# Seven block products for eight in the down product's middle twelve K tiles

## The chip, the cores and the metric

The kernel runs on one core of one Trainium2 chip. The metric is the device time of one execution in microseconds, given as the median of several runs. The profile is one execution taken by the hardware profiler. PE is the matrix engine (TensorE), DVE the vector engine, ACT the scalar engine, POOL the GpSimd engine, and SP the engine that issues all transfers here, in one queue.

## The reference

One layer of an encoder over 1088 tokens (64 sample tokens and 1024 of a prompt): a combined projection, windowed attention beside a state-space mixer, an output projection and LN1, and then a gated feed-forward part and LN2. The change lies in the feed-forward part:

```
h = layer_norm(DN_ALPHA * x + mix, ln1_g, ln1_b)
g, up = jnp.split(h @ w_gate_up, 2, axis=-1)
f = (jax.nn.silu(g) * up) @ w_down
y = layer_norm(DN_ALPHA * h + f, ln2_g, ln2_b)
```

The model width is 1024 (8 tiles of 128 features), the hidden width 2816 (22 tiles of 128). Everything is fp32.

## The kernel before, in words

Features lie on the 128 partitions and tokens on the free axis; the 1088 tokens are four chunks of 272 (`QN`). To keep fp32 accuracy every operand is split into h, its rounding to the matrix engine's fp32r format (a copy on ACT), and l, the rest (a subtraction on DVE, both in `split`, line 1307). A product is then three matmuls, h x h, h x l and l x h (`mm3`, line 758, and `acc3`).

Nothing is issued as the program text has it. All instructions are recorded by `Plan` (from line 90), with the row buffers and banks that they use. `order` (line 285) then writes each engine's queue: of the instructions that are ready by its cost table it takes the earliest, and among those the one of the lowest priority number, which grows with the place in the text (times `step`) and falls with the cost of all that hangs on it. `plan.base` shifts that number. The queues are fixed after that, and an instruction waits in its queue for what it needs.

Buffers: `R` hands out 21 row buffers of 1088 words, `W` ten weight buffers of 1024 words, `R4` four big buffers of four rows each, and `PM` the eight PSUM banks.

The gate/up stage (`gu_load`, line 1372, and `gu_mm`, line 1405) already uses seven products for eight: a hidden tile's gate and up weights, each cut into two halves of four K tiles, are the 2x2 blocks of the left side, and h, cut by the same halves and by pairs of token chunks, those of the right. h is mixed once (`h_mix`, line 1330); its products 7, 6 and 4 keep twelve row buffers to the end of the stage. The weights are mixed per tile: `ws` and `wt` hold the sums s1 to s4, and of u's second half `wd` is made. The product order is 1, 5, 2, 7, 3, 6, 4 (`ORDER`), each for the chunk pairs s = 0 and 1. Products 1 and 2 share bank A, 5 and 3 bank D, 7 and 4 bank C. The tile's activation `act` is stored to DRAM (`ascr`), 22 in all.

The down stage runs over K in four blocks of 5, 5, 4 and 8 hidden tiles (`DN_BLOCKS`, line 39). `act_load` (line 1449) reads the activations back and splits them. For each of eight output tiles `mo` and four chunks `c`, `down` (line 1463) sums its K tiles in one bank, and one DVE instruction adds the bank to the result f (in the queues: `g0_0` and so on, chunk and feature half), which begins as ALPHA times h.

The last block runs chunk by chunk, so that LN2 of a chunk (`fm_norm`, line 1197) goes beside the matmuls of the next. For chunk c it sums over features with `mu` and `va` on PE, and spreads the scale over the partitions with three matmuls `rp` (`spread`, line 1190). Chunk 3 has its own end (`fm_tail`, line 1227): it subtracts a mean of the first five feature tiles (`shl`), adds the other three tiles' products to that, and forms the statistics `dcl` (mean by token), `del` (the same, spread) and `val` (squares) in pieces:

```
        plan.base = TAILB
        token_rows(dc, ds, True, False)
        PE.matmul(de[:, 0:n], omean, ds, start=True, stop=False)
        token_rows(va, B, True, False)
        token_rows(dc, d[7], False, True)
        token_rows(va, q[7], False, True)
        PE.matmul(de[:, 0:n], omean, d[7], start=False, stop=True)
```

Here ds is the sum of d[5] and d[6], made by DVE, and B the sum of the squares q[0] to q[6], made by POOL; both lie in the buffer `ntl`.

Of the kernel before, what the change touches and what calls it, by code (L numbers as in the profile page):

```python
# [10 lines left out]
F32 = mybir.dt.float32  # L11
# [27 lines left out]
DN_BLOCKS = [5, 5, 4, 8]  # L39
# [50 lines left out]
class Plan:  # L90
# [194 lines left out]
    def order(self):  # L285
# [13 lines left out]
        step = 1.1 * sum(o.cost for o in ops if o.eng == "PE") / n  # L299
# [121 lines left out]
def layer(ctx: ExitStack, tc: tile.TileContext, I, O):  # L421
# [13 lines left out]
    def R(dt, name, words=1088):  # L435
        return own(row.tile([128, words], dt, tag="R", name=name), "R", NR)
# [68 lines left out]
    ascr = [DT([128, T], f"ascr{m}") for m in range(DFF_T)]  # L505
    kscr = DT([16, 32, 128], "kscr")
# [720 lines left out]
    def fm_tail(c, gg, bbias, step):  # L1227
# [41 lines left out]
        token_rows(va, q[7], False, True)  # L1269
        PE.matmul(de[:, 0:n], omean, d[7], start=False, stop=True)  # L1270
# [100 lines left out]
    @plan.part  # L1371
    def gu_load(m):
        g, u = R(F32, f"wg{m}"), R(F32, f"wu{m}")
        for i, t in enumerate((g, u)):
            SP.dma_start(t[:, 0:1024], I["w_gu"][2 * m + i].rearrange("p a b -> p (a b)"))
        a11, a12, a21, a22 = g[:, 0:512], g[:, 512:1024], u[:, 0:512], u[:, 512:1024]
        sa, sb = R(F32, f"ws{m}"), R(F32, f"wt{m}")
        s1, s2, s3, s4 = sa[:, 0:512], sa[:, 512:1024], sb[:, 0:512], sb[:, 512:1024]
        V.tensor_tensor(s1, a21, a22, op=ALU.add)
        V.tensor_tensor(s2, s1, a11, op=ALU.subtract)  # L1380
        V.tensor_tensor(s3, a11, a21, op=ALU.subtract)
        V.tensor_tensor(s4, a12, s2, op=ALU.subtract)
# [22 lines left out]
    def gu_mm(m, subs):  # L1405
# [36 lines left out]
        if 1 in subs:  # L1442
            SP.dma_start(ascr[m], act)
# [4 lines left out]
    @plan.part  # L1448
    def act_load(m0, nb, big):
        for i in range(nb):  # L1450
            a = R(F32, f"ar{m0 + i}")
            SP.dma_start(a, ascr[m0 + i])
            if big:
                if i % 2 == 0:
                    t_ = R4(F32R, f"ah{m0 + i}")
                h, l = t_[:, 2 * (i % 2)], t_[:, 2 * (i % 2) + 1]
            else:
                h, l = R(F32R, f"ah{m0 + i}"), R(F32R, f"al{m0 + i}")
            split(a, h, l)
            ACT_[m0 + i] = (h, l)  # L1460

# [109 lines left out]
    m0 = 0  # L1571
    for bi, nb in enumerate(DN_BLOCKS):
        act_load(m0, nb, bi % 2 == 1)
        if bi + 1 < len(DN_BLOCKS):
            for mo in range(8):
                down(m0, nb, bi == 0, mo, dn_load(m0, nb, mo))
        else:
            wd = [dn_load(m0, nb, mo, W if mo < 4 else RW) for mo in range(8)]
            for c in range(4):
                if c == 3:  # L1580
                    fm_tail(c, g2, b2, lambda k, f: down(m0, nb, False, k, wd[k], (c,), f))
                    break
                for mo in range(8):
                    down(m0, nb, False, mo, wd[mo], (c,))
                fm_norm(1, c, g2, b2, ln2_out)
        m0 += nb
# [94 lines left out]
```

## Time and profile before

| what | us |
|---|---|
| runs (three) | 1162.64 to 1166.91, median 1166.75 |
| the profiled execution's own time | 1167.67 |
| its span on the core | 1165.9 |
| PE busy | 1121.4 |
| DVE busy | 758.0 |
| ACT busy | 488.2 |

The span is the time from the first to the last instruction of the core; some 1.8 us of the execution lie around it. The mean granted clock of PE is 0.986 of full speed. A matmul's record lasts longer than the distance to the next one, since matmuls are pipelined, so durations of PE are read as distances between starts.

### The profile page before, as it was taken

How to read it: one execution, taken by the hardware profiler on the slowest of the kernel's cores; microseconds unless marked ns; L12 is line 12 of the kernel's file. 1: busy time of each engine (PE TensorE's matmuls, PEld its weight loads, DVE VectorE, ACT ScalarE, POOL GpSimd, SP SyncE). 2: the span in 40 equal slices, each digit the busy share in tenths (PEclk: the TensorE clock that was granted, in tenths of full speed). 3: DMA queues.
4: the chain of work that ended last, by engine and by line, in shares of the span. 5: the costliest groups of instructions: out<-in, count | busy, mean ns of one | idle time of the engine just before them, and what ended most of it. 6: DMA issues, size and time to landing. Idle time of an engine off the chain costs nothing.

```text
span 1165.9 us, 21135 instructions
## 1 busy us (share of the span) xinstructions
PE 1121.4 (96%) x8595; PEld 1093.7 (94%) x8595; DVE 758.0 (65%) x1550; ACT 488.2 (42%) x989; POOL 78.6 (7%) x123
## 2 busy tenths in 40 slices
PE   5998898999999999999999999999999999999996
PEld 5998788798799999999999999999999999999995
DVE  7999995677866998564645646556447353743554
ACT  5557345785832565243333333333334121410334
POOL 1101012123310010000000000000000000000012
PEclk8999999999999999999999999999999999999997
DMA  9455578420120322141131221311367161410112
GB/s 298 112 151 159 165 224 243 124 86 10 39 76 14 112 95 94 56 167 56 56 112 56 87 80 56 111 56 69 120 211 244 35 230 46 154 38 1 40 39 77
DMA packets 73721, 122.50 MB, mean 105 GB/s; under 512 B 11974, under 2 KB 49416, under 8 KB 73608
## 3 DMA queue, kind: packets, MB, share of 16 engines
q1 hardware_dynamic: 73624, 121.16, 32.1%
q8 instruction: 67, 1.10, 0.4%
q14 instruction: 30, 0.25, 0.1%
HBM read 84.08 MB, written 38.24 MB: 105 GB/s over the span
## 4 chain that ended last, share of the span: by engine, by line
PE 62%; DVE 2%; POOL 1%; DMA 0%; issue 0%; ACT 0%; POOLq 0%; DVEq 0%; ACTq 0%
PE dn L417 22%; PE guA L417 10%; PE guD L417 10%; PE guC L417 10%; PE guB L417 5%; PE gp L417 3%; DVE dl L417 1%; DVE f L417 1%; DMA ar<-ascr 0%; POOL rs L417 0%; PE rp L417 0%; DVE nt L417 0%; POOL ntl L417 0%; PE val L417 0%; PE mu L417 0%
## 5 line engine op out<-in xcount | busy, mean ns | idle before, releaser
L417 PE MATMUL guA<-hc,wah 128*128 128x272 f32 x640 | 127.1, 288 | 0.0
L417 DVE TENSOR_TENSOR tm<-tm 128x272 f32<-128x272 f32 x80 | 35.0, 438 | 122.5 <-ACT tm L417 122.5
L417 PEld LDWEIGHTS guA<-hc,wah 128*128 128x128 f32 x640 | 100.5, 188 | 0.0
L417 PE MATMUL guA<-hc,wal 128*128 128x272 f32 x320 | 92.4, 289 | 0.0
L417 DVE TENSOR_TENSOR g<-g,dn 128x272 f32<-128x272 f32 x93 | 40.1, 435 | 78.4 <-PE dn L417 78.0
L417 PE MATMUL guC<-hh,wd 128*128 128x272 f32 x320 | 64.0, 289 | 0.0
L417 PE MATMUL guD<-hc,wch 128*128 128x272 f32 x320 | 63.1, 287 | 0.0
L417 PE MATMUL guD<-hc,wbh 128*128 128x272 f32 x320 | 62.8, 289 | 0.0
L417 PEld LDWEIGHTS guA<-hc,wal 128*128 128x128 f32 x320 | 60.2, 188 | 0.0
L417 POOL TENSOR_TENSOR rs<-rs,nhalf 128x3 f32<-128x3 f32 x7 | 7.8, 1113 | 772.2 <-DVE rs L417 772.2
L417 PEld LDWEIGHTS guC<-hh,wd 128*128 128x128 f32 x320 | 51.6, 188 | 0.0
L417 DVE TENSOR_TENSOR wcl<-wt,wch 128x1024 fp32r<-128x1024 f32 x20 | 24.5, 1225 | 39.9 <-PE guD L417 38.2
L417 PEld LDWEIGHTS guD<-hc,wbh 128*128 128x128 f32 x320 | 50.4, 188 | 0.0
L417 PEld LDWEIGHTS guD<-hc,wch 128*128 128x128 f32 x320 | 50.2, 188 | 0.0
L417 ACT ACTIVATE act<-guA 128x272 f32<-128x272 f32 x40 | 15.9, 397 | 79.5 <-PE guA L417 79.5
L417 PE MATMUL guD<-hc,wbl 128*128 128x272 f32 x160 | 46.4, 290 | 0.0
L417 PE MATMUL guB<-hl,wbh 128*128 128x272 f32 x160 | 46.3, 289 | 0.0
L417 PE MATMUL guC<-hl,wd 128*128 128x272 f32 x160 | 46.2, 289 | 0.0
L417 PE MATMUL guC<-hl,wch 128*128 128x272 f32 x160 | 46.2, 289 | 0.0
L417 PE MATMUL guB<-hh,wbl 128*128 128x272 f32 x160 | 46.2, 289 | 0.0
L417 PE MATMUL guC<-hh,wch 128*128 128x272 f32 x160 | 46.1, 288 | 0.0
L417 PE MATMUL guD<-hc,wcl 128*128 128x272 f32 x160 | 46.0, 288 | 0.0
(618 smaller groups left out, 3868.7 us busy)
## 6 DMA issues: line engine op xcount, KB each, us to landing
ascr<-act SPq DMA_DIRECT2D x22, 544.0 KB, 3.1
ar<-ascr SPq DMA_DIRECT2D x22, 544.0 KB, 4.8
wg<-in_w_gu SPq DMA_DIRECT2D x20, 512.0 KB, 4.6
wu<-in_w_gu SPq DMA_DIRECT2D x20, 512.0 KB, 4.5
f<-xscr SPq DMA_DIRECT2D x8, 544.0 KB, 5.5
xscr<-f SPq DMA_DIRECT2D x8, 544.0 KB, 3.2
g<-xscr SPq DMA_DIRECT2D x8, 544.0 KB, 5.1
x<-in_xt SPq DMA_DIRECT2D x8, 512.0 KB, 11.5
```

The lines of the kernel that those rows point to most:

```text
L417: real(*a, **k)
```

## The change

K tiles 4 to 15 (`DN0`, `DN1`) are no longer multiplied plainly. Two neighbouring hidden tiles 2i and 2i+1, each cut into token chunks of two kinds, e = 0 and 1, are the 2x2 blocks of the right side; the left side's are two neighbouring output tiles 2p and 2p+1 by two pairs of K tiles. `a_mix` takes a pair of hidden tiles as soon as gate/up has made them, forms the seven mixed blocks, splits each and stores h and l side by side in one DRAM row (`hscr`), 42 in all; these twelve tiles aren't stored to `ascr`. `mix_load` reads them back as matmul operands without a further split (`bm`), two pairs of hidden tiles at a time. `dn_mix_load` reads the weights of a block (2 output tiles by 4 K tiles), forms the sums and splits them. `dn_mix` issues the seven products of a block for both s, each 2 x 3 matmuls per s: 84, where the plain form has 2 x 4 x 4 x 3 = 96. There are three groups of K tiles by four pairs of output tiles. DVE adds the banks to f and to a running sum u (`us`), which after the last group is added to three blocks of f.

K is now cut 4 (plain), 12 (mixed), 6 (plain, chunk by chunk). The weights of the last block are loaded by `dn_pair_load`, two output tiles in three buffers. In gate/up the weights of tile m+1 are recorded before the matmuls of m, the sums s3 and s4 are formed in place (one buffer less), and the last tile's two halves are recorded one behind the other. In `fm_tail` the statistics are recorded in another order, and POOL's sum leaves out q[6], which `val` takes by itself. `step` becomes a constant.

```diff
-        step = 1.1 * sum(o.cost for o in ops if o.eng == "PE") / n
+        step = 193.7
...
-            if k < 7:
+            if k < 6:
                 P_.tensor_tensor(B, B, q[k], op=ALU.add)
+        plan.base = 0
+        token_rows(dc, ds, True, False)
+        token_rows(va, B, True, False)
+        token_rows(va, q[6], False, False)
         plan.base = TAILB
-        token_rows(dc, ds, True, False)
+        token_rows(dc, d[7], False, True)
+        plan.base = 0
         PE.matmul(de[:, 0:n], omean, ds, start=True, stop=False)
-        token_rows(va, B, True, False)
-        token_rows(dc, d[7], False, True)
+        PE.matmul(de[:, 0:n], omean, d[7], start=False, stop=True)
+        plan.base = TAILB
         token_rows(va, q[7], False, True)
-        PE.matmul(de[:, 0:n], omean, d[7], start=False, stop=True)
...
+    def a_mix(i):
...
+        def put(n, x):
+            t = R(F32R, f"am{i}_{n}")
+            h, l = (t[:, 2 * QN * j:2 * QN * j + 2 * QN] for j in range(2))
+            split(x, *(y.rearrange("p (s n) -> p s n", s=2) for y in (h, l)))
+            SP.dma_start(hscr[i, n], f32(t))
+
+        put("1", b11)
+        V.tensor_tensor(b11, b12, b11, op=ALU.subtract)
+        put("5", b11)
+        put("2", b21)
+        V.tensor_tensor(b12, b22, b12, op=ALU.subtract)
+        put("7", b12)
+        put("3", b22)
+        V.tensor_tensor(b22, b22, b11, op=ALU.subtract)
+        put("6", b22)
+        V.tensor_tensor(b21, b21, b22, op=ALU.subtract)
+        put("4", b21)
...
+    def dn_mix_load(i0, p):
...
+        V.tensor_tensor(s1, a21, a22, op=ALU.add)
+        V.tensor_tensor(s2, s1, a11, op=ALU.subtract)
+        V.tensor_tensor(a21, a11, a21, op=ALU.subtract)
+        V.tensor_tensor(s4, a12, s2, op=ALU.subtract)
...
+    def dn_mix(i0, p, w, first, last):
...
+                for i in range(2):
...
+                    with plan.group():
+                        PE.matmul(o, wh, mh, start=new and i == 0, stop=False, skip_group_check=True)
+                        PE.matmul(o, wh, ml, start=False, stop=False, skip_group_check=True)
+                        PE.matmul(o, wl, mh, start=False, stop=fin, skip_group_check=True)
...
+                if n == "1":
+                    if first:
+                        S_.activation(u, o, AF.Copy)
+                    else:
+                        add(u)
+                elif n in "57":
+                    add(f22)
+                elif n == "2":
+                    add(f11)
+                elif n == "3":
+                    add(f12)
+                elif n == "4":
+                    add(f21)
+                else:
+                    add(u)
+                    if last:
+                        plan.base = 100
+                        for f in (f12, f22, f21):
+                            V.tensor_tensor(f, f, u, op=ALU.add)
+                        plan.base = 0
...
-    gu_mm(2, (0, 1))
-    for m in range(3, DFF_T):
-        gu_load(m)
-        gu_mm(m, (0, 1))
+    for m in range(2, DFF_T):
+        if m + 1 < DFF_T:
+            gu_load(m + 1)
+        for s in ((0, 1),) if m + 1 < DFF_T else ((0,), (1,)):
+            gu_mm(m, s)
+        if DN0 <= m < DN1 and m % 2:
+            a_mix(m // 2)
+    act_load(0, [None, None] + bigs("ah0"))
...
+    for i in range(DN0 // 2, DN1 // 2, 2):
+        mix_load(i)
+        for p in range(4):
+            dn_mix(i, p, dn_mix_load(i, p), i == DN0 // 2, i == DN1 // 2 - 2)
+    m0, nb = DN1, DFF_T - DN1
```

The change moves instructions in all queues from gate/up on. Three places matter here.

ACT at the start of hidden tile 6. `wah7` and `wbh7` are weights of tile 7, `act5` the activation of tile 5, and `tm6_0` and `tm6_1` take products 1 (bank A) and 5 (bank D) of tile 6. Before:

```order
L417 ACTIVATE wah7_902<-wg7_898 128x1024
L417 ACTIVATE act5_865<-act5_865 128x272 x2
L417 ACTIVATE wbh7_904<-ws7_900 128x1024
L417 ACTIVATE tm6_0_889<-guA6_0_888 128x272
L417 ACTIVATE tm6_1_891<-guA6_1_890 128x272
L417 ACTIVATE tm6_0_889<-guD6_0_892 128x272
L417 ACTIVATE tm6_1_891<-guD6_1_893 128x272
```

Nothing but weights and one activation stands between the copies. With the change, `am2_2` and so on are the mixed blocks of tiles 4 and 5:

```order
L420 ACTIVATE wah7_934<-wg7_931 128x1024
L420 ACTIVATE am2_2_926<-act5_913 128x544
L420 ACTIVATE am2_3_928<-act5_913 128x544
L420 ACTIVATE am2_7_927<-act4_892 128x544
L420 ACTIVATE tm6_0_943<-guA6_0_942 128x272
L420 ACTIVATE tm6_0_943<-guD6_0_946 128x272
L420 ACTIVATE wbh7_936<-ws7_933 128x1024
L420 ACTIVATE am2_6_929<-act5_913 128x544
L420 ACTIVATE tm6_1_945<-guA6_1_944 128x272
L420 ACTIVATE am2_4_930<-act5_913 128x544
```

Three copies of the mixed activations now stand ahead of the first copy out of tile 6's banks, and two more among the following ones.

DVE while the matrix engine is in the third K block (before) and in the third of the last four mixed blocks (now). Before, each bank (`dn10`, the block of K tiles 10 to 13, by output tile and chunk) is read once, by an add to the result `g`:

```order
L417 TENSOR_TENSOR g0_0_1228<-g0_0_1228,dn10_3_0_1403 128x272
L417 TENSOR_TENSOR g1_0_1229<-g1_0_1229,dn10_3_1_1404 128x272
L417 TENSOR_TENSOR g2_0_1230<-g2_0_1230,dn10_3_2_1405 128x272
L417 TENSOR_TENSOR g3_0_1231<-g3_0_1231,dn10_3_3_1406 128x272
L417 TENSOR_TENSOR g0_1_1232<-g0_1_1232,dn10_4_0_1409 128x272
L417 TENSOR_TENSOR g1_1_1233<-g1_1_1233,dn10_4_1_1410 128x272
L417 TENSOR_TENSOR g2_1_1234<-g2_1_1234,dn10_4_2_1411 128x272
L417 TENSOR_TENSOR g3_1_1235<-g3_1_1235,dn10_4_3_1412 128x272
```

These are eight adds of one size, in the order in which PE ends the banks.

With the change, `dmD6_2_0` is bank D of the mixed block of output tiles 4 and 5 at s = 0; `wrl6_3` and `wml6_3` are weights of the next block:

```order
L420 TENSOR_TENSOR g1_1_1306<-g1_1_1306,dmD6_2_0_1531 128x272
L420 TENSOR_TENSOR g3_1_1308<-g3_1_1308,dmD6_2_1_1532 128x272
L420 TENSOR_TENSOR wrl6_3_1540<-wr6_3_1537,wrh6_3_1539 128x1024
L420 TENSOR_TENSOR g1_1_1306<-g1_1_1306,dmC6_2_0_1533 128x272
L420 TENSOR_TENSOR g0_1_1305<-g0_1_1305,dmA6_2_0_1529 128x272
L420 TENSOR_TENSOR wml6_3_1542<-wm6_3_1538,wmh6_3_1541 128x768
L420 TENSOR_TENSOR g3_1_1308<-g3_1_1308,dmC6_2_1_1534 128x272
L420 TENSOR_TENSOR g2_1_1307<-g2_1_1307,dmA6_2_1_1530 128x272
L420 TENSOR_TENSOR g1_1_1306<-g1_1_1306,dmD6_2_0_1531 128x272
L420 TENSOR_TENSOR g1_0_1302<-g1_0_1302,us0_1371 128x272
L420 TENSOR_TENSOR us1_1400<-us1_1400,dmB6_2_0_1535 128x272
L420 TENSOR_TENSOR g2_0_1303<-g2_0_1303,us0_1371 128x272
```

The adds of one block, weight splits of the next, and closing adds of the running sum `us0` from the block before follow one another in one queue.

The end of chunk 3, PE before, where `dn14_7_3` is the last output tile's product and `dl1` and `ql1` are d[7] and q[7]:

```order
L417 MATMUL dcl_1524<-omean_80,ntl_1512 128x1 x3
L417 MATMUL del_1523<-ntl_1512,omean_80 128x272
L417 MATMUL dn14_7_3_1529<-ah18_1438,wd14_7h_1465 128x272 x2
L417 MATMUL dn14_7_3_1529<-ah18_1438,wd14_7l_1466 128x272
L417 MATMUL val_1525<-omean_80,ntl_1512 128x1 x3
L417 MATMUL dn14_7_3_1529<-ah20_1441,wd14_7h_1465 128x272 x2
L417 MATMUL dn14_7_3_1529<-ah20_1441,wd14_7l_1466 128x272
L417 MATMUL dn14_7_3_1529<-ah20_1441,wd14_7h_1465 128x272 x2
L417 MATMUL dn14_7_3_1529<-ah20_1441,wd14_7l_1466 128x272
L417 MATMUL dcl_1524<-omean_80,dl1_1514 128x1 x3
L417 MATMUL val_1525<-omean_80,ql1_1516 128x1 x3
```

The statistics of `ntl` stand among the last products. DVE there, before:

```order
L417 TENSOR_TENSOR dl1_1514<-dl1_1514,dn14_6_3_1528 128x272
L417 TENSOR_TENSOR ntl_1512<-dl1_1514 128x272
L417 TENSOR_TENSOR dl1_1514<-dl1_1514,dn14_7_3_1529 128x272
L417 COPY rsl_1530<-dcl_1524 128x3
L417 TENSOR_TENSOR rsl_1530<-rsl_1530,dcl_1524 128x3
L417 SCALAR_TENSOR_TENSOR rsl_1530<-val_1525,rsl_1530 128x3
```

The last add (of `dn14_7_3`) stands right behind the sum `ntl`. PE with the change:

```order
L420 MATMUL dn16_7_3_1645<-al21_1562,wl3_b_1579 128x272
L420 MATMUL dn16_7_3_1645<-ah21_1561,wl3_b_1579 128x272
L420 MATMUL dcl_1640<-omean_80,ntl_1628 128x1 x2
L420 MATMUL val_1641<-omean_80,ntl_1628 128x1
L420 MATMUL dcl_1640<-omean_80,ntl_1628 128x1
L420 MATMUL val_1641<-omean_80,ntl_1628 128x1 x2
L420 MATMUL dcl_1640<-omean_80,dl1_1630 128x1 x3
L420 MATMUL val_1641<-omean_80,ql1_1632 128x1 x6
L420 MATMUL del_1639<-ntl_1628,omean_80 128x272
```

The statistics now all follow the last product. DVE with the change:

```order
L420 TENSOR_TENSOR dl1_1630<-dl1_1630,dn16_6_3_1644 128x272
L420 TENSOR_SCALAR nt12_1621<-ident_75,rs12_1626 128x128
L420 TENSOR_TENSOR ntl_1628<-dl1_1630 128x272
L420 TENSOR_SCALAR nt12_1621<-ident_75,rs12_1626 128x16
L420 TENSOR_TENSOR g2_0_1303<-g2_0_1303,rp2_1627 128x1088
L420 TENSOR_TENSOR dl1_1630<-dl1_1630,dn16_7_3_1645 128x272
L420 TENSOR_TENSOR g2_1_1307<-g2_1_1307,rp2_1627 128x1088
L420 COPY rsl_1646<-dcl_1640 128x3
L420 TENSOR_TENSOR rsl_1646<-rsl_1646,dcl_1640 128x3
L420 SCALAR_TENSOR_TENSOR rsl_1646<-val_1641,rsl_1646 128x3
```

Here two parts of chunk 2's scale (`nt12`) and its two multiplies `g2` stand around the last add.

## Rows read from the trace of the kernel before

**Rows 1.** The page: busy time (share) and instructions by engine; the chain's shares.
```profile
PE 1121.4 (96%) x8595; PEld 1093.7 (94%) x8595; DVE 758.0 (65%) x1550; ACT 488.2 (42%) x989; POOL 78.6 (7%) x123
...
PE 62%; DVE 2%; POOL 1%; DMA 0%; issue 0%; ACT 0%; POOLq 0%; DVEq 0%; ACTq 0%
PE dn L417 22%; PE guA L417 10%; PE guD L417 10%; PE guC L417 10%; PE guB L417 5%; PE gp L417 3%; DVE dl L417 1%; DVE f L417 1%; DMA ar<-ascr 0%; POOL rs L417 0%; PE rp L417 0%; DVE nt L417 0%; POOL ntl L417 0%; PE val L417 0%; PE mu L417 0%
```

**Rows 2.** Stages: window, length, busy us (count) by engine, PEclk, DMA share, GB/s.
```profile
600.00:700.00 100.00, 100.00 (x798) 100.00 (x797) 53.47 (x92) 35.54 (x67) 0.00 (x0) 1.00 0.23 82
900.00:950.00 50.00, 50.00 (x400) 50.00 (x400) 21.62 (x38) 9.36 (x11) 0.00 (x0) 1.00 0.40 131
940.00:960.00 20.00, 20.00 (x162) 20.00 (x161) 12.25 (x20) 6.68 (x7) 0.00 (x0) 1.00 0.73 273
```

**Rows 3.** The chain in order of time: start, length, what; two tiles of gate/up.
```profile
621.83 2.25 PE guA L417 x18
...
642.92 2.25 PE guA L417 x18
```

**Rows 4.** DVE in order of time, gate/up: start, length, instruction, idle time before it.
```profile
701.21 1.23 DVE L417 TENSOR_TENSOR wcl<-wt,wch 128x1024 fp32r<-128x1024 f32 x1 [2.27 <-PE guD L417]
702.35 0.43 DVE L417 TENSOR_TENSOR tm<-tm,guB 128x272 f32<-128x272 f32 x1
702.70 0.69 DVE L417 TENSOR_TENSOR wd<-wu,wd 128x512 fp32r<-128x512 f32 x1
703.30 0.43 DVE L417 TENSOR_TENSOR act<-tm,guD 128x272 f32<-128x272 f32 x1
703.64 0.44 DVE L417 TENSOR_TENSOR tm<-tm 128x272 f32<-128x272 f32 x1
...
706.60 0.72 DVE L417 TENSOR_TENSOR act<-act,tm 128x544 f32<-128x544 f32 x1
707.24 0.43 DVE L417 TENSOR_TENSOR tm<-tm,guC 128x272 f32<-128x272 f32 x1
```

**Rows 5.** Groups from 900 us on: busy us, mean ns of one, idle before.
```profile
L417 DVE TENSOR_TENSOR g<-g,rp 128x1088 f32<-128x1088 f32 x6 | 7.5, 1285 | 1.3 <-PE rp L417 1.3
```

**Rows 6.** Groups of ACT, 540 to 860 us.
```profile
L417 ACT ACTIVATE wd<-wu 128x512 fp32r<-128x512 f32 x15 | 9.5, 632 | 43.0 <-PE guD L417 43.0
```

**Rows 7.** The page: DMA issues, KB each, median us to landing.
```profile
ascr<-act SPq DMA_DIRECT2D x22, 544.0 KB, 3.1
ar<-ascr SPq DMA_DIRECT2D x22, 544.0 KB, 4.8
```

**Rows 8.** PE in order of time, the last chunk.
```profile
1139.11 0.62 PE L417 MATMUL shl<-ntl,oks 128*128 128x272 f32 x2
...
1145.00 0.29 PE L417 MATMUL dn<-ah,wd_7l 128*128 128x272 f32 x1
1146.05 0.80 PE L417 MATMUL dcl<-omean,ntl 128*128 128x1 f32 x6 [0.76 <-DVE ntl L417]
...
1149.08 0.83 PE L417 MATMUL val<-omean,ntl 128*128 128x1 f32 x6 [1.29 <-POOL ntl L417]
...
1150.72 0.43 PE L417 MATMUL dn<-ah,wd_7l 128*128 128x272 f32 x1
```

**Rows 9.** DVE in order of time, the last chunk.
```profile
1139.76 4.97 DVE L417 TENSOR_TENSOR dl<-g,shl 128x272 f32<-128x272 f32 x8 [1.80 <-PE shl L417]
1144.65 0.77 DVE L417 TENSOR_TENSOR dl<-dl,dn 128x272 f32<-128x272 f32 x2
...
1151.19 0.44 DVE L417 TENSOR_TENSOR dl<-dl,dn 128x272 f32<-128x272 f32 x1 [5.29 <-PE dn L417]
1153.16 0.16 DVE L417 COPY rsl<-dcl 128x3 f32<-128x3 f32 x1 [1.53 <-PE dcl L417]
```

More of the change, by code (lines that the diff above doesn't have):

```diff
@@ L505, in layer @@
     ascr = [DT([128, T], f"ascr{m}") for m in range(DFF_T)]
+    hscr = {(i, n): DT([128, T], f"hscr{i}_{n}") for i in range(DN0 // 2, DN1 // 2) for n in "1234567"}
     kscr = DT([16, 32, 128], "kscr")
@@ L1442, in gu_mm @@
         if 1 in subs:
-            SP.dma_start(ascr[m], act)
+            if not DN0 <= m < DN1:
+                SP.dma_start(ascr[m], act)
+    @plan.part
+    def a_mix(i):
+        ab = [ACT_[2 * i + j].rearrange("p (s e n) -> p e s n", s=2, e=2) for j in range(2)]
+        b11, b12, b21, b22 = ab[0][:, 0], ab[0][:, 1], ab[1][:, 0], ab[1][:, 1]
+        def put(n, x):
[14 more added lines that the diff above has]
+        put("4", b21)
     def dn_load(m0, nb, mo, T_=None):
@@ L1460, in act_load, with bigs, mix_load @@
             ACT_[m0 + i] = (h, l)
+    def bigs(name):
+        t = R4(F32R, name)
+        return [(t[:, 2 * i], t[:, 2 * i + 1]) for i in range(2)]
+    BM, US = {}, {}
+    @plan.part
+    def mix_load(i0):
+        t4 = [R4(F32R, f"bm{i0 + j}") for j in range(2)]
+        for x, n in enumerate(ORDER):
+            for j in range(2):
+                t = t4[j][:, x] if x < 4 else R(F32R, f"bm{i0 + j}_{n}")
+                SP.dma_start(f32(t), hscr[i0 + j, n])
+                for s in range(2):
+                    BM[i0 + j, n, s] = tuple(t[:, QN * (2 * y + s):QN * (2 * y + s) + QN] for y in range(2))
@@ new lines, in dn_mix @@
+    @plan.part
+    def dn_mix(i0, p, w, first, last):
+        bank = {}
+        if first and p % 2 == 0:
+            US[p // 2] = R(F32, f"us{p // 2}")
+        for n in ORDER:
+            b = {"1": "A", "2": "A", "5": "D", "3": "D", "7": "C", "4": "C", "6": "B"}[n]
+            for s in range(2):
+                new = (b, s) not in bank
+                if new:
+                    bank[b, s] = PM(f"dm{b}{i0}_{p}_{s}")[:, 0:QN]
+                o = bank[b, s]
+                for i in range(2):
+                    wh, wl = w[n][i]
+                    mh, ml = BM[i0 + i, n, s]
+                    fin = (not new or b == "B") and i == 1
+                    with plan.group():
+                        PE.matmul(o, wh, mh, start=new and i == 0, stop=False, skip_group_check=True)
+                        PE.matmul(o, wh, ml, start=False, stop=False, skip_group_check=True)
+                        PE.matmul(o, wl, mh, start=False, stop=fin, skip_group_check=True)
+                u = US[p // 2][:, QN * (2 * (p % 2) + s):QN * (2 * (p % 2) + s) + QN]
+                f11, f12, f21, f22 = (fq(2 * s + e, 2 * p + m) for m in range(2) for e in range(2))
+                add = lambda f: V.tensor_tensor(f, f, o, op=ALU.add)
+                if n == "1":
[18 more added lines that the diff above has]
+                        plan.base = 0
@@ L1565, in layer @@
     h_mix(1)
[L1566 to L1586 removed]
+    for m in range(2, DFF_T):
[6 more added lines that the diff above has]
+    act_load(0, [None, None] + bigs("ah0"))
+    x0_load((0, 1), "g")
+    for mo in range(8):
+        down(0, DN0, True, mo, dn_load(0, DN0, mo))
+    for i in range(DN0 // 2, DN1 // 2, 2):
[3 more added lines that the diff above has]
+    m0, nb = DN1, DFF_T - DN1
+    act_load(m0, bigs("ah1") + bigs("ah2") + [None] * (nb - 4))
+    wd = []
+    for p in range(4):
+        wd += dn_pair_load(m0, p, RW if p == 3 else W)
+    for c in range(4):
+        if c == 3:
+            fm_tail(c, g2, b2, lambda k, f: down(m0, nb, False, k, wd[k], (c,), f))
+            break
+        for mo in range(8):
+            down(m0, nb, False, mo, wd[mo], (c,))
+        fm_norm(1, c, g2, b2, ln2_out)
     plan.order()
```

78 lines of the change are left out of this document (56 added, 22 removed).

## The prediction

> **What bounds the kernel now.** I read the busy times first, then the chain of waits, then the stages. The matrix engine PE is busy for 1121.4 of 1165.9 us, and the chain that ended last is 62% PE, led by the group dn (the down product) with 22% [rows 1]. A busy PE can still be badly fed, so I look at its pace. From the third hidden tile on, one tile of the gate/up stage follows another every 642.92 - 621.83 = 21.09 us [rows 3]; such a tile is 7 x 2 x 4 x 3 = 168 matmuls, so one 128x272 matmul costs 0.1255 us, start to start. The down stage keeps the same pace: 400 matmul records fall in 50 us [rows 2], two of them counted from the edges, which is 0.1256. In both stages PE is busy for the whole window while VectorE (DVE) is busy for 53.5 of 100 us and then 21.6 of 50, and the transfers take 0.23 and 0.40 of their time [rows 2]. So here PE's instruction count is the time, and whatever DVE, ACT and the DMA queues do is cover, until they run out of room.
>
> **What the change removes.** Twelve of 22 K tiles go from eight block products to seven. Plain, they are 12 x 8 x 4 x 3 = 1152 matmuls; mixed, 12 blocks of 84 = 1008. The 144 that go have the same shape and pace, 144 x 0.1255 = 18.1 us. For the sum I split them at one matmul, shl of the last chunk: the last K block has six tiles in place of eight, so that 54 down matmuls follow shl in the old order and 42 in the new one. 132 matmuls therefore go ahead of shl, and **shl comes 132 x 0.1255 = 16.6 us sooner**.
>
> **Behind shl.** Now, shl starts at 1139.11 and the span ends 26.8 us later [rows 8]. Its 54 matmuls are worth 6.8 us, but the last one starts at 1150.72, 11.6 us after shl: PE stands in front of dcl until 1146.05 and of val until 1149.08 [rows 8], since these statistics stand in its queue ahead of the last twelve down matmuls. In the new order they all follow the last one. What PE now meets instead is rp2, the scale of chunk 2, two of whose parts wait for DVE, which does the eight dl subtractions first. Those last 4.97 us from 0.65 us after shl, two adds take 0.77 us more [rows 9], and the scale's last part and the sum ds end some 7.2 us after shl; PE issues the third rp2 at 7.4 and the last six matmuls by 8.2. On DVE one multiply of chunk 2 (1.28 us, [rows 5]) then stands ahead of the last add, which ends at about 9.4 us. In the old run it ends at 1151.63, 12.5 us after shl [rows 9]. That is **3.1 us**. The second multiply of chunk 2 comes between this add and the statistics' reader; DVE idled 1.53 us there [rows 9], which covers it. Bounds: all of PE's stall goes (11.6 - 6.8 = 4.8 us gained), or the two multiplies cost in full while only dcl's 0.76 us wait goes (2 x 1.28 - 0.76 = 1.8 us lost). I take 3.1, worked out along the queue, as nearer to the upper row.
>
> **What the change adds to DVE.** A consecutive DVE instruction starts before the previous one is over in the trace: 702.35, 702.70, 703.30, 703.64 are starts of instructions that last 0.43, 0.69, 0.43 us [rows 4]. Start to start 272 elements cost 0.345, 512 cost 0.60, 544 cost 0.64, 1024 cost 1.14; on that line 256 are 0.33, 768 are 0.87 and 1088 are 1.21 us. A mixed block needs four 256-wide sums and two weight splits (4 x 0.33 + 1.14 + 0.87 = 3.3 us) and 14 adds from PSUM (4.8 us, 12 of them in the first four blocks): 8.2 us beside 84 x 0.1255 = 10.5 us of PE. The tight place is the last four blocks. Between the first read of their PSUM and the first read of the last K block, DVE's new order holds 101 instructions: 72 of 272 (18 of the 24 closing adds among them), 13 of 256, six activation splits of 1088, and five, three and two of 512, 768 and 1024. That is 44.3 us against 4 x 10.5 = 42.2 of PE. All twelve blocks have 105.9 against 126.5. So DVE falls at most 2.1 us behind, and only if nothing was done ahead.
>
> [...]
>
> **What it adds to the gate/up stage.** Six times, for a pair of hidden tiles, seven splits (ACT 0.63 us for 512 [rows 6], DVE 0.64) and four subtractions: 11 x 0.64 = 7.0 us of DVE in 42.2, on top of 0.53 busy; that makes 0.70. ACT goes from 0.36 to about 0.46. Both stay cover. The weight loads move one tile ahead, the sums of a tile use one row buffer less, and the stores grow by five of 544 KB per pair; stores land in 3.1 us [rows 7]. **Cost zero**, if ACT is never held by a row buffer (third rival).
>
> **What it adds to the transfers.** 42 mixed tiles come back in place of 12 plain ones. From the first down matmul to the last mixed one PE works 384 + 1008 matmuls, 174.8 us. In this time 42 x 557 KB and some 15 MB of weights and plain tiles, 38 MB, must come: 218 GB/s. The old run moved 273 GB/s over 940 to 960 us with 0.73 of the engines busy [rows 2] and PE never waited, so I count this as hidden.
>
> **Sum.** For all new stalls together I take **2.0 us**, the excess of the last four blocks; the ends are 0 and what the first rival gives. The profiled span goes from 1165.9 by -16.6 - 3.1 + 2.0 = -17.7 to 1148.2 us. That execution took 1167.67 us, 0.9 above the median of the runs, 1166.75; the median goes to **1149 us**.
>
> **Rivals.**
> *DVE paces the last four mixed blocks* by its full durations, each some 0.09 us above the distance of starts (0.43 against 0.345, 1.23 against 1.14 [rows 4]): 44.3 + 101 x 0.09 = 53.4 against 42.2 us, 11.2 in place of 2.0, thus 1158 us. It decides once back-to-back adds come slower than about 0.33 us each. For it: PE may run ahead only by eight PSUM banks, and each is emptied by DVE alone, in its queue's order, among weight splits. Against it: starts 0.345 us apart. [...] 0.12.
> *Transfers pace the mixed blocks; slower than before.* A loaded tile took 4.8 us from issue to landing [rows 7]. If the 42 came one behind another, they would need 201.6 us where PE gives 174.8: 26.8 us of stall, 1149 - 2 + 26.8 = 1174. It decides below the 218 GB/s above, or where a buffer is free only one at a time. Against: 273 GB/s with several under way. 0.04.
> *The gain is given back in gate/up.* Twelve of 21 row buffers stay with the mixed h; act, tm and the next weights take six or seven, so the mixed activations find two or three. On ACT three of their copies stand ahead of the copy of product 1, which frees the bank for product 2, 48 matmuls (6.0 us) after the tile begins. If one waits for a store (3.1 us [rows 7]) with no slack left, PE loses that in each of six pairs: 18.6 us, 1168, no difference. Against: the six microseconds, and ACT two-thirds idle. 0.08.
> *It does not take work off PE.* The counts in the new queue exclude that; only another unknown mishap is left, 0.04 with either sign.
>
> **How the numbers follow.** My forecast has 0.72. About 0.5% (5.8 us) is what a measurement of this kernel can tell from no change, so faster means below 1160.9. Forecast and first rival lie there, with half of the unknown: 0.72 + 0.12 + 0.02 = 0.86. The gate/up rival is no change, with 0.01 of the unknown: 0.09. Slower keeps 0.05. The range reaches down to no stall and the whole of the tail's stall (1149 - 2.0 - 1.7 = 1145.3) and up to the first rival (1158, and half a microsecond for the head's few exchanged DVE instructions): 1145 to 1158.5, which leaves out some 0.16.
>
> **What would show it.** Right: 8595 - 144 + 6 = 8457 matmul records (the six are three more column sums of val, which the page counts twice); PE busy throughout gate/up and all mixed blocks, with 10.5 us from a block to the next; DVE above 0.8 busy there; the last down matmul about 8 us after shl, and the end near 23.7 us after it. Wrong: PE idle before dmA or dmD with DVE as the releaser (first rival); idle at bm with a DMA as the releaser (second); PE idle at guA's second product, with ACT's am copies behind DMA waits (third); a gap at rp2 above 2 us (the tail).

## The result, and the profile after

The changed kernel takes 1148.65 us (median of four runs, 1146.06 to 1149.74), the kernel before 1165.67 in the same series; the ratio is 0.9855, with a 95% interval of 0.9837 to 0.9872, so 14.9 to 19.0 us are gained. Predicted was 1149, in a range of 1145 to 1158.5. The profiled execution took 1147.59 us with a span of 1145.8. Below, one of ten runs of plain12 (1222.79 us, mean granted clock 0.847 where the others have 0.984 to 0.991) is left out of its median as slow.

From the page of the changed kernel, the busy times, the shares of the chain and the two new transfers answer to [rows 1, 7]:

```profile
PE 1103.5 (96%) x8457; PEld 1076.6 (94%) x8457; DVE 862.7 (75%) x1788; ACT 506.4 (44%) x1035; POOL 77.5 (7%) x122
...
PE 60%; DVE 4%; issue 0%; POOL 0%; POOLq 0%; DVEq 0%
...
hscr<-am SPq DMA_DIRECT2D x42, 544.0 KB, 3.4
bm<-hscr SPq DMA_DIRECT2D x42, 544.0 KB, 10.0
```

The 8457 matmul records are those that were forecast; DVE is busier by 105 us and PE less by 18. The chain is still PE, with the mixed products (dmA and so on) in the place of part of dn. Now the stages (window, length, busy us of PE, its weight loads, DVE, ACT and POOL, granted clock, DMA share, GB/s): gate/up, the first four plain tiles, and the twelve mixed blocks.

```profile
443.43:871.46 428.03, 428.03 (x3410) 428.03 (x3410) 289.92 (x474) 175.60 (x331) 0.00 (x0) 1.00 0.36 130
871.46:919.69 48.23, 48.23 (x386) 48.23 (x386) 24.64 (x50) 6.92 (x9) 0.00 (x0) 1.00 0.81 308
919.69:1046.00 126.31, 126.15 (x1007) 125.84 (x1007) 107.12 (x241) 30.37 (x37) 0.00 (x0) 1.00 0.48 171
```

PE is never idle in the first two and for 0.16 us in the third, which lasts 126.3 us, 10.5 for each of twelve blocks. DVE is at 0.85 there, and the transfers at 0.48 after a peak of 308 GB/s ahead of it. To see which term of the sum came true, I cut both spans at three starts on PE: the first matmul of the gate/up stage (guA), the first of the down product (dn) and shl of the last chunk. The starts of the first two, from the views of tile and time, before:

```profile
L417 PE MATMUL guA<-hc,wah x640: 282/288/296, 446.9 to 865.1; 128*128 128x272 f32 x160
```
```profile
874.77 0.29 PE L417 MATMUL dn<-ah,wd_0h 128*128 128x272 f32 x1
```

and after:

```profile
L420 PE MATMUL guA<-hc,wah x640: 282/288/293, 443.3 to 866.5; 128*128 128x272 f32 x160
```
```profile
871.30 0.29 PE L420 MATMUL dn<-ah,wd_0h 128*128 128x272 f32 x1
```

| stretch, us | before | after | forecast | measured |
|---|---|---|---|---|
| start to guA | 446.9 | 443.3 | 0 | -3.6 |
| guA to dn | 427.9 | 428.0 | 0 | +0.1 |
| dn to shl | 264.3 | 247.0 | -14.6 | -17.3 |
| shl to the end | 26.8 | 27.5 | -3.1 | +0.7 |

The total is right, and it is so because two misses of opposite sign nearly cancel: the middle gained more than was forecast, and the end gained nothing. The 3.6 us ahead of guA turn out not to belong to the change (below).

From the first guA to shl PE waits in one place only (engine, releaser: us in total, times, longest). It waits for DVE in the mixed blocks, and the timeline shows all that this costs:

```profile
PE dmA L420 <- DVE us L420: 0.2, 1, 0.2
```
```profile
1038.39 0.29 PE L420 MATMUL dmC<-bm,wrl 128*128 128x272 f32 x1
1038.84 0.52 PE L420 MATMUL dmA<-bm,wrh 128*128 128x272 f32 x2 [0.16 <-DVE us L420]
```

From 1038.39 to 1038.84 a step takes 0.45 in place of 0.1255 us, and the next one 0.11 more: 0.43 us is the whole stall, where 2.0 stood in the sum and 11.2 in the first rival. DVE does fall behind. It reads the first bank of the ninth block at 1005.31 and the first of the last K block at 1051.24, which is 45.9 us (1.2 of them idle) for 101 instructions, where PE needs 42.2. The last mixed bank is emptied at 1054.98, 8.9 us after PE started its last mixed matmul (1046.11); PE had other banks to work in meanwhile and did not wait:

```profile
1005.31 0.43 DVE L420 TENSOR_TENSOR us<-us,dmA 128x272 f32<-128x272 f32 x1
...
1051.24 0.42 DVE L420 TENSOR_TENSOR g<-g,dn 128x272 f32<-128x272 f32 x1
...
1054.98 0.42 DVE L420 TENSOR_TENSOR g<-g,dmC 128x272 f32<-128x272 f32 x1
```

Besides the 132 matmuls, six others left the stretch ahead of shl: those that spread chunk 2's scale (rp), 0.58 us to the next matmul in the kernel before (1134.36 to 1134.94). With the change the first of them starts 1.2 us after shl.

```profile
1134.36 0.73 PE L417 MATMUL rp<-nt,omean 128*128 128x128 f32 x6
```

The last chunk on PE answers to [rows 8]:

```profile
1118.29 0.62 PE L420 MATMUL shl<-ntl,oks 128*128 128x272 f32 x2
...
1124.77 0.49 PE L420 MATMUL rp<-nt,omean 128*128 128x128 f32 x2 [1.55 <-DVE nt L420]
...
1126.72 0.34 PE L420 MATMUL dn<-ah,wl_b 128*128 128x272 f32 x1
1126.86 0.85 PE L420 MATMUL dcl<-omean,ntl 128*128 128x1 f32 x4
...
1128.42 0.99 PE L420 MATMUL val<-omean,ntl 128*128 128x1 f32 x4
1129.28 1.42 PE L420 MATMUL dcl<-omean,dl 128*128 128x1 f32 x6
1130.56 2.70 PE L420 MATMUL val<-omean,ql 128*128 128x1 f32 x12
1133.12 1.25 PE L420 MATMUL del<-ntl,omean 128*128 128x272 f32 x2
1134.16 1.11 PE L420 MATMUL del<-dl,omean 128*128 128x272 f32 x2
```

and on DVE to [rows 9]:

```profile
1127.41 0.43 DVE L420 TENSOR_TENSOR dl<-dl,dn 128x272 f32<-128x272 f32 x1
...
1130.73 0.16 DVE L420 COPY rsl<-dcl 128x3 f32<-128x3 f32 x1 [1.69 <-PE dcl L420]
```

The last down matmul starts 8.4 us behind shl and the last add ends at 9.55; 8.2 and 9.4 were forecast. But dcl takes what this add makes only at 11.0, since PE is at the statistics of ntl until then, and behind it stand twice as many column sums of val as before and del's matmul of ntl.

### The profile page after: what moved, and what is told of

Same layout as the page of the kernel before. It is cut to its first block, busy times and chain, and to the rows that moved or that the text cites. A ratio compares the mean times of both kernels' runs of the same rounds, so it can differ in the third digit from the quotient of the medians.

```text
span 1145.8 us, 21257 instructions
## 1 busy us (share of the span) xinstructions
PE 1103.5 (96%) x8457; PEld 1076.6 (94%) x8457; DVE 862.7 (75%) x1788; ACT 506.4 (44%) x1035; POOL 77.5 (7%) x122
## 4 chain that ended last, share of the span: by engine, by line
PE 60%; DVE 4%; issue 0%; POOL 0%; POOLq 0%; DVEq 0%
PE guD L420 11%; PE guA L420 11%; PE guC L420 11%; PE dn L420 10%; PE guB L420 5%; PE gp L420 3%; PE dmA L420 3%; PE dmD L420 2%; PE dmC L420 2%; PE dmB L420 1%; DVE g L420 1%; DVE dl L420 1%; DVE f L420 1%; DVE nt L420 0%; DVE us L420 0%
## 5 line engine op out<-in xcount | busy, mean ns | idle before, releaser
L420 PE MATMUL guC<-hl,wch 128*128 128x272 f32 x320 | 92.4, 289 | 0.0
L420 PE MATMUL guC<-hh,wcl 128*128 128x272 f32 x320 | 92.2, 288 | 0.0
L420 PE MATMUL guC<-hh,wch 128*128 128x272 f32 x320 | 92.2, 288 | 0.0
L420 PE MATMUL guD<-hc,wd 128*128 128x272 f32 x480 | 73.7, 287 | 0.0
L420 PEld LDWEIGHTS guD<-hc,wd 128*128 128x128 f32 x480 | 65.3, 188 | 0.0
L420 PEld LDWEIGHTS guC<-hh,wch 128*128 128x128 f32 x320 | 60.3, 188 | 0.0
L420 PEld LDWEIGHTS guC<-hl,wch 128*128 128x128 f32 x320 | 60.3, 188 | 0.0
L420 PEld LDWEIGHTS guC<-hh,wcl 128*128 128x128 f32 x320 | 60.2, 188 | 0.0
L420 DVE TENSOR_TENSOR wcl<-wu,wch 128x1024 fp32r<-128x1024 f32 x20 | 24.5, 1225 | 39.3 <-PE guD L420 39.3
L420 ACT ACTIVATE wrh<-wr 128x1024 fp32r<-128x1024 f32 x12 | 12.7, 1061 | 92.0 <-DVE wr L420 55.3
```

What stands on the lines that cost most here:

```text
L420: real(*a, **k)
```

## The experiments

Times are medians. The other columns are distances on PE in the profiled run, as above; "add" and "del" are the ends of the last add and of del, counted from shl.

| kernel | time | ratio to before (interval) | guA starts | guA to dn | dn to shl | add | del | shl to end |
|---|---|---|---|---|---|---|---|---|
| before | 1165.67 | | 446.9 | 427.9 | 264.3 | 12.5 | 16.4 | 26.8 |
| after | 1148.65 | 0.9855 (0.9837 to 0.9872) | 443.3 | 428.0 | 247.0 | 9.55 | 17.0 | 27.5 |
| after_again | 1147.28 | 0.9835 (0.9817 to 0.9854) | 443.9 | 428.0 | 246.9 | 9.56 | 16.1 | 26.5 |
| plain12 | 1166.50 | 1.0015 (1.0000 to 1.0029) | 444.3 | 427.9 | 264.6 | 9.57 | 16.9 | 27.9 |
| dve8 | 1162.51 | 0.9975 (0.9960 to 0.9990) | 442.9 | 428.0 | 261.8 | 9.58 | 17.0 | 27.4 |
| gu_old | 1182.97 | 1.0152 (1.0133 to 1.0170) | 447.1 | 460.7 | 246.6 | 9.88 | 17.6 | 28.0 |
| gu_late | 1184.12 | 1.0166 (1.0129 to 1.0202) | 443.2 | 463.2 | 246.5 | 9.56 | 16.2 | 26.8 |
| rows19 | 1182.13, one run | | 475.8 | 430.5 | 246.4 | 9.56 | 17.0 | 27.4 |
| tail_new_on_before | 1164.22, one run | | 442.7 | 427.9 | 265.7 | 7.77 | 15.7 | 26.1 |
| tail_old | 1146.87 | 0.9841 (0.9820 to 0.9862) | 445.8 | 428.0 | 246.2 | 12.4 | 16.6 | 27.1 |
| tail_q6 | 1146.67 | 0.9840 (0.9818 to 0.9861) | 442.8 | 428.0 | 246.4 | 9.91 | 16.3 | 26.7 |
| tail_best | 1144.53 | 0.9827 (0.9804 to 0.9850) | 449.1 | 428.0 | 246.7 | 8.15 | 13.6 | 24.1 |
| tail_best_again | 1144.92 | 0.9825 (0.9805 to 0.9846) | 445.8 | 428.0 | 246.2 | 8.15 | 13.5 | 24.0 |

**plain12: the mix alone undone.**

```diff
-    for i in range(DN0 // 2, DN1 // 2, 2):
-        mix_load(i)
-        for p in range(4):
-            dn_mix(i, p, dn_mix_load(i, p), i == DN0 // 2, i == DN1 // 2 - 2)
+    for m0 in (4, 8, 12):
+        act_load(m0, bigs(f"ap{m0}") + bigs(f"aq{m0}"))
+        for mo in range(8):
+            down(m0, 4, False, mo, dn_load(m0, 4, mo))
```

(`a_mix` goes too, and all tiles are stored to `ascr`.)

> The changed kernel with its twelve middle K tiles multiplied plainly, in three blocks of four; gate/up's new order, the last block of six tiles and the new tail stay. Theory (the gain is the 144 matmuls, less 0.4 us of new stall): 1148.7 + 18.1 - 0.4 = 1166.3 us, ratio to before 1.000. Rival (some 3.5 us of the gain come from the head, where the profiled run of the changed kernel was 3.6 us ahead when gate/up began): 1163 us, ratio 0.997.

1166.50 came, and 17.6 us between dn and shl: 144 x 0.1255 = 18.1 less the stall of 0.43. So all of the gain is the 144 matmuls; the other edits together bring nothing that this measurement can tell (1.0015 of the kernel before; if anything they cost a little).

**after_again: the changed kernel once more.**

> The changed kernel as it is, beside the next one on the same chip. Theory: 1148.5 us, within 2; the first start of guA moves by some us from run to run, the distance from it to the end stays at 702.5 us within 0.5. Rival (the 3.6 us by which gate/up began sooner in the profiled run come from the change): guA's first matmul near 443.3 us again.

The distance from guA to the end is 701.5, not within 0.5 of 702.5: 1.0 us of it lies behind shl. guA starts at 443.9 here, which by itself would speak for the rival. But the table has the answer: the kernel before and tail_new_on_before have the same queues on every engine up to the down stage, and guA starts at 446.9 in one and 442.7 in the other; tail_best, twice the same program, on two chips, starts it at 449.1 and 445.8. The 3.6 us are inside what differs from run to run.

**dve8: eight more DVE instructions in each mixed block.**

```diff
                 else:
                     add(u)
+                if n in "5637":
+                    x = {"5": f22, "7": f22, "2": f11, "3": f12, "4": f21, "6": u}[n]
+                    V.tensor_tensor(x, x, x, op=ALU.max)
+                if n == "6":
```

> The changed kernel with eight more DVE instructions of 128x272 in each of the twelve mixed blocks (a tile compared with itself after the adds of products 5, 6, 3 and 7; values stay the same). By the distances of starts DVE's queue then holds 77.6 us of work in the first eight mixed blocks, against 84.3 us of PE, and 57.4 in the last four (138 instructions), against 42.2. Theory (DVE is cover until its distances of starts exceed PE's, 0.345 us each): nothing in the first eight, about 14 us of PE idle in the last four with DVE as releaser, total 1162.5 us. Rival 1 (each DVE instruction costs its full duration, 0.43): some 12 us more again, 1174 or above. Rival 2 (DVE has room to spare there): under 3 us, 1151 or below.

1162.51 came, and 14.8 us between dn and shl. The first eight blocks, the last four, and what follows them (windows as above), and PE's waits from 915 to 1070 us:

```profile
919.00:1004.00 85.00, 84.58 (x676) 84.30 (x674) 81.71 (x208) 14.45 (x21) 0.00 (x0) 1.00 0.50 182
1004.00:1050.00 46.00, 42.90 (x331) 41.77 (x331) 45.52 (x116) 14.28 (x16) 0.00 (x0) 1.00 0.37 129
1050.00:1062.00 12.00, 5.93 (x29) 5.49 (x28) 12.00 (x19) 2.52 (x4) 0.00 (x0) 0.75 0.25 84
```
```profile
PE dn L420 <- DVE wl_c L420: 6.1, 1, 6.1
PE dmA L420 <- DVE wrl L420: 1.2, 1, 1.2
```

In the first stretch PE loses 0.4 us though DVE is busy for 81.7 of 85 (66.9 in the changed kernel); in the second DVE is full and PE starts to wait; most is lost at the first plain tile behind, whose weights DVE splits late. From the first read of the ninth block's banks to the first of the last K block DVE's queue holds 138 instructions in place of 101, and they take 58.9 us in place of 45.9. So DVE is cover about as far as the sum of its distances of starts goes, as the prediction counted them, and not as far as the sum of full durations, by which some 12 us more would have been lost. That the total came out to the decimal is luck: about 14 us of idle PE were expected, and there are five waits of 9.6 in all (the three that are not shown are 0.9, 0.9 and 0.5); 3 us more lie in the low granted clock behind (0.75 over 12 us). The changed kernel stands just at that edge.

**gu_old and gu_late: gate/up's own edits undone.** gu_old takes back the order of recording and the in-place sums, gu_late the order alone (the last hunk):

```diff
-        sa = R(F32, f"ws{m}")
+        sa, sb = R(F32, f"ws{m}"), R(F32, f"wt{m}")
...
     for m in range(2, DFF_T):
-        if m + 1 < DFF_T:
-            gu_load(m + 1)
+        if m > 2:
+            gu_load(m)
```

> The changed kernel with gate/up's own edits undone: weights of a tile recorded right ahead of its matmuls, the sums s3 and s4 in a buffer of their own (one row buffer more per tile); the mixed activations stay. Theory (gate/up's new order is cover with room to spare): gate/up keeps 21.09 us per hidden tile, total within 2 us of 1148.7. Rival (the third rival's mechanism is real and was cured by these edits): PE waits for copies on ACT that a row buffer holds back, 3 us or more in each of six pairs, 1167 us or above.

> The changed kernel with only the recording order of gate/up's weights undone (a tile's weights right ahead of its matmuls); the sums stay in place, with one row buffer less per tile. In gu_old, with both undone, the stage from the first to the last start of guA's matmuls took 455.8 us in place of 423.3, with two waits of PE at the start of each tile that follows a pair. Theory (the order is the cause: weight sums and splits of the next tile stand behind the pair's mixed activations on DVE): most of it stays, stage 445 us or more, total 1172 us or above. Rival (the extra row buffer was the cause): stage within 3 us of 423.3, total 1148 to 1152.

Both stages grow, by 32.6 and 35.2 us, and both kernels are slower than before: the order alone is enough. What the further row buffer would cost by itself was not run. PE's waits in gu_old and then in gu_late, from 440 to 910 us:

```profile
PE guA L420 <- ACT tm L420: 13.8, 6, 2.3
PE guA L420 <- DVE wal L420: 6.7, 6, 1.1
```
```profile
PE guD L420 <- DVE wbl L420: 8.2, 6, 1.4
PE guD L420 <- ACT wbh L420: 7.1, 6, 1.2
PE guA L420 <- DVE wal L420: 6.7, 6, 1.1
```

Six waits of each kind: one set at the start of the tile behind each pair. What releases them in gu_old, on DVE, ACT and PE at one such tile:

```profile
541.18 1.36 DVE L420 TENSOR_TENSOR am<-act,am 128x544 fp32r<-128x544 f32 x2
...
543.06 0.68 DVE L420 TENSOR_TENSOR wt<-wg,wu 128x512 f32<-128x512 f32 x1
```
```profile
543.86 0.40 ACT L420 ACTIVATE tm<-guA 128x272 f32<-128x272 f32 x1 [1.89 <-DVE wt L420]
```
```profile
544.31 0.82 PE L420 MATMUL guA<-hc,wah 128*128 128x272 f32 x2 [2.31 <-ACT tm L420]
```

The tile's weight sums ws and wt stand on DVE behind the pair's am splits. ACT's copy tm out of product 1's bank waits 1.89 us for wt's sum, and PE 2.31 us for that copy. It is a row buffer that tm waits for: in gu_old as it is built, tm (s = 0) of each of these six tiles is given the buffer in which the tile's wu lay, and this sum is the last instruction that reads wu. So the third rival's mechanism is real, at its place on ACT, but the buffer is held by a sum on DVE and not by a store. In gu_late this wait is down to 1.2 us in six, and PE waits for the late weights themselves instead. PE's waits add up to 20.5 and 23.2 us, so 12 more are lost in either case. Most of it is the granted clock, in gu_old ahead of and behind the wait:

```profile
540.00:546.00 6.00, 3.69 (x23) 3.47 (x23) 6.00 (x11) 3.68 (x6) 0.00 (x0) 0.86 0.51 201
546.00:549.00 3.00, 3.00 (x20) 3.00 (x19) 3.00 (x4) 1.90 (x4) 0.00 (x0) 0.72 1.02 328
```

PE goes on at a mean clock of 0.72: from 544.93 to 547.20 ten matmuls start 0.227 us apart, in place of 0.1255. Ten microseconds around each of the six places (540 to 550 and so on) have a mean of 0.83 in gu_old, by my estimate 1.7 us lost each time and 10.2 in all (by the starts at the first place, 15 matmuls take 3.50 us, 544.31 to 547.81, in place of 1.88: 1.6 lost); in gu_late four of the six have 0.83, 6.8 us in all, and two have 1.00. The stage's mean is 0.98 over 461.9 us in gu_old and 0.99 over 464.0 in gu_late. The rest is mainly that a wait counts from the end of the last record, 0.16 us after the moment at which the next matmul would have started (a record of 0.29 us, starts 0.1255 apart): 12 waits in gu_old make 2.0 us, 24 in gu_late 3.9. That leaves 1.3 us of gu_late without a name. So PE pays here for the pause and then again for the slow clock: by these numbers the second payment is half the first in gu_old and three tenths of it in gu_late.

**rows19: two row buffers fewer.**

```diff
-NR, NW = 21, 10
+NR, NW = 19, 10
```

> The changed kernel with 19 row buffers in place of 21, in the whole program; what counts is the gate/up stage, from the first matmul of guA to the first of the down product (428 us in the changed kernel). Theory (the mixed activations have two or three buffers, stores land in 3.4 us, so two fewer leave at most one and ACT's copies wait for stores): gate/up grows by 3 us or more in each of six pairs, 18 us or more. Rival (row buffers are not short in gate/up at all): 428 us again, within 2.

Gate/up takes 430.5 us, 2.5 more, a little outside the 2 that the rival allowed; the theory of a shortage, 18 us or more, falls. The kernel loses 32.5 us ahead of guA, which starts at 475.8. The planner had free hands to write another order, so this says that gate/up can live with 19, not that the queue of the changed kernel could.

**The end of the last chunk.** tail_new_on_before puts the new order of `fm_tail` into the kernel before (that hunk of the change's diff, alone), and tail_old puts the old one into the changed kernel:

```diff
-            if k < 6:
+            if k < 7:
...
-        plan.base = 0
+        plan.base = TAILB
         token_rows(dc, ds, True, False)
+        PE.matmul(de[:, 0:n], omean, ds, start=True, stop=False)
         token_rows(va, B, True, False)
-        token_rows(va, q[6], False, False)
...
```

tail_q6 gives q[6] back to POOL, and tail_best also moves chunk 2's scale (`last2`):

```diff
-            if k < 6:
+            if k < 7:
                 P_.tensor_tensor(B, B, q[k], op=ALU.add)
...
-        token_rows(va, q[6], False, False)
...
         rp = PB(f"rp{c}")[:, 0:n]
+        last2 = gi == 1 and c == 2
+        plan.base = 90 if last2 else 0
         spread(rp, dg, rs[:, 4:7])
+        plan.base = -100 if last2 else 0
```

> The kernel before with only the new order of the last statistics. There the 54 down matmuls follow shl without a wait for a chunk's scale, the last ends some 7.5 us after shl and the last add on DVE some 8. Theory (PE's queue of statistics behind the last down matmul sets the end, at the low granted clock): val waits for POOL's sum until some 9 us, the end comes 26.5 to 28 us after shl, no sooner than the 26.8 of the old order by more than half a us. Rival (the prediction's step: the last add sets the end, which follows it by 14.3 us): 22 to 23 us after shl.

> Only the end of the last chunk goes back to the old order of the statistics (sums of the first seven squares on POOL, dcl and del of ntl ahead of the last six down matmuls). In the changed kernel the span ends 27.5 us after shl starts. Theory (PE's queue of statistics behind the last down matmul sets the end): three column sums of val and one del matmul leave that queue, so the end comes 25 to 26.5 us after shl. Rival (the prediction's step: the last add on DVE sets the end, and the old order makes PE wait for DVE): the last add moves from 9.5 to 11 us or later behind shl, and the end to 29 us or more. Time of the whole kernel within 2 us of 1148.7 by either.

> The changed kernel, but POOL adds the square of feature tile 6 again and val doesn't take it by itself; the order of the rest as the planner gives it. Theory (PE's statistics set the end): three column sums of 0.45 us go, the end comes 26.1 us after shl in place of 27.5. Rival 1 (the last add sets it): 27.5, no change. Rival 2 (POOL's sum is late, which is why it was cut): PE waits for it ahead of val, end at 28 us or more.

> As tail_q6, and the last two parts of chunk 2's scale stand behind the last down matmul, so that PE doesn't wait for them among the last down matmuls, and the last add stands ahead of chunk 2's multiplies on DVE. Theory (PE's queue sets the end): the statistics start 1.1 us sooner and are 1.35 us shorter, the end comes about 25.1 us after shl in place of 27.5, the time is 1146.3. Rival (the end hangs on what comes behind del: DVE's subtractions and multiplies): less than 1 us of this arrives, end after 26.5 us or more.

> tail_best once more, beside the changed kernel on the same chip. Theory: the 3.4 us that its profile shows behind shl arrive in the time, 1145 us. Rival (they are taken back elsewhere, by the stores of chunk 2 or the clock): within 1 us of the changed kernel.

The clearest is tail_new_on_before. The last add ends at 7.8 us in place of 12.5, and the end comes at 26.1 in place of 26.8. PE there:

```profile
1136.31 0.62 PE L417 MATMUL shl<-ntl,oks 128*128 128x272 f32 x2
...
1143.31 0.29 PE L417 MATMUL dn<-ah,wd_7l 128*128 128x272 f32 x1
...
1145.45 0.38 PE L417 MATMUL val<-omean,ntl 128*128 128x1 f32 x2 [1.51 <-POOL ntl L417]
...
1147.33 2.70 PE L417 MATMUL val<-omean,ql 128*128 128x1 f32 x12
```

4.7 us of a sooner last add bring 0.7 us, since PE works through its queue of statistics from 1145.45 on without a gap. The rival's 22 to 23 are far off; 26.1 lies a little below the theory's 26.5 to 28. tail_old says it the other way round: the last add is 2.8 us later than in the changed kernel, and the end is not. Its 27.1 lies above my 25 to 26.5 and far below the rival's 29, and tail_q6's 26.7 is 0.8 better, not 1.35. By the end alone neither can be told from the changed kernel itself, whose queue ended at 27.5 and 26.5 us in two runs, and in plain12 and gu_late, which share it, at 27.9 and 26.8. What differs between the two runs is the granted clock; the changed kernel first, then after_again:

```profile
1124.30:1126.90 2.60, 1.99 (x14) 1.77 (x15) 2.11 (x5) 0.68 (x2) 0.91 (x1) 0.98 0.00 0
1126.90:1128.40 1.50, 1.50 (x9) 1.50 (x9) 1.50 (x3) 0.81 (x2) 0.00 (x0) 0.50 0.00 0
```
```profile
1118.80:1127.40 8.60, 6.90 (x54) 6.39 (x52) 7.66 (x15) 2.93 (x7) 4.41 (x6) 1.00 0.00 0
1127.40:1128.90 1.50, 1.50 (x14) 1.50 (x13) 1.50 (x3) 0.82 (x2) 0.00 (x0) 0.79 0.00 0
```

It falls from 1.00 to 0.50, behind a wait of 1.55 us for rp, 8.5 us after shl in the one and about 9.5 in the other; in the kernel before it was about 11 (0.62 from 1150.00 to 1150.70, 0.50 from there on). Three column sums take 0.66 us at a clock of 1.00 (dcl of ntl in the kernel before starts at 1146.05 [rows 8], and del behind it at 1146.71) and 1.28 at 0.50 (1129.28 to 1130.56 above). So the sooner finish of the down matmuls also moved more of the statistics under the clock of 0.50.

Seven profiles share the changed kernel's queues behind shl. In gu_old, the changed kernel, rows19, dve8, plain12, gu_late and after_again the clock falls 7.8, 8.5, 8.6, 8.6, 8.7, 9.4 and 9.5 us after shl, and the end comes at 28.0, 27.5, 27.4, 27.4, 27.9, 26.8 and 26.5. Beside those with nearly the same moment, tail_q6 (8.6, end 26.7) is 0.7 to 1.2 us sooner, and tail_old (7.4, end 27.1) 1.0 sooner than gu_old, the nearest. So a shorter queue on PE does seem to bring the end forward, by about 1 us, which the moment of the clock hides; these are single profiles.

tail_best is beyond that scatter: no wait for rp among the last down matmuls, three column sums fewer, and the end at 24.1 and 24.0.

```profile
1123.91 0.62 PE L420 MATMUL shl<-ntl,oks 128*128 128x272 f32 x2
...
1129.43 0.29 PE L420 MATMUL dn<-ah,wl_b 128*128 128x272 f32 x1
...
1134.07 1.42 PE L420 MATMUL val<-omean,ql 128*128 128x1 f32 x6
...
1136.39 1.11 PE L420 MATMUL del<-dl,omean 128*128 128x272 f32 x2
```

Its theory asked for 25.1. The clock falls 9.6 and 9.7 us after shl there; after_again, with 9.5, ended at 26.5, so 2.5 us are the edits'. From guA to the end it takes 698.8 and 698.2 us against 702.5 and 701.5. Its time beside the changed kernel on one chip is 1144.92 against 1147.28; the two ratios' intervals overlap, so the 3 us are shown in the profile and only likely in the time. It is the fastest version found.

## Why the prediction was right, and where it was not

- **PE bounds it, and the gain is the matmuls.** Right. 144 matmuls at 0.1255 us are the gain, as plain12 shows by itself.
- **132 of them ahead of shl, 16.6 us, with 2.0 us of new stalls.** The mechanism was right, the stall mis-sized: 0.43 us. The count of DVE's work held (45.9 us against 44.3 forecast), but the sum took its lag for idle time of PE, and the banks let PE run on. Of the remaining 1.1 us, some 0.6 were short gaps in the old kernel's first down tiles (at 877.8 to 881.5 us, where the distances are up to 0.23 us too long), and 0.6 are chunk 2's six rp matmuls, which the sum had not moved. Tenths are those of one profile: in tail_new_on_before, with the old queue, this stretch took 265.7 us and not 264.3.
- **Behind shl, 3.1 us.** This step failed. The last add was forecast within 0.2 us, but it was taken for what sets the end. The measured 27.5 is 23.7 plus 1.44 (dcl waits for PE's statistics of ntl, from the add at 9.55 to 10.99), 1.28 (val's three more column sums) and 1.04 (del of ntl, 1133.12 to 1134.16), by the rows of this one profile; no run takes the three apart. The prediction named the new order and counted the three column sums among the records, and gave all of it no time.
- **Gate/up at cost zero.** The number was right. The reason (cover with room to spare) was not: without the weights recorded one tile ahead, the pair's mixing costs 33 to 35 us, more than all that the change brings. The third rival was priced at 18.6 us from one wait of 3.1 per pair; the waits were 3.4 to 3.9, and the low clock added 10.2 and 6.8 us by the estimate above.
- **First rival, DVE by full durations.** It did not happen: 0.43 us of stall, not 11.2. The starts in the trace of the kernel before are 0.345 us apart where an instruction lasts 0.43 [rows 4], and in the changed kernel the 101 instructions took 45.9 us, not the 53.4 of full durations.
- **Second rival, transfers.** PE never waits for bm. The loads take 10.0 us each to land, but several are under way at once: all 42 are issued from 859.1 to 1001.2, in 142 us, where one behind another they would need 420. No run here took this cover away.

## What to carry to other kernels

Follow the end of a kernel along every engine's queue: an operand that comes sooner is worth little while the engine that takes it is still at other work (4.7 us brought 0.7 in tail_new_on_before), and "this stands behind that now" has a price of its own. An edit that looks like housekeeping (weights one tile ahead) can be what lets another be free, so price a change with and without it. And cut the span at fixed instructions before comparing two profiles, since the stretch ahead of them differed by 6 us (442.8 in tail_q6, 449.1 in tail_best) between kernels whose queues are the same there.

## What was not expected of the hardware

Short waits of PE cost more than themselves here. Waits of 1.1 and 2.3 us at six hidden tiles of gu_old added up to 20.5 us and cost 32.6, with a granted clock of 0.72 behind the first of the longer ones (546.00 to 549.00); in gu_late the clock was below 1.00 at four of the six tiles only (0.83 over ten microseconds); in the last chunk of the changed kernel one wait of 1.55 us was followed by a clock of 0.50, and the moment at which it fell differed by up to 1.7 us between seven profiles of one queue and moved the end with it.
